# MLP entry of a hybrid encoder layer: the per-row scalars of the norm move off GpSimd, and one form of the residual rows is kept instead of two

## The chip, the core and the metric

One core of a Trainium2 chip runs the whole program. The engines are named as the profile names them: PE (TensorE matmul, with PEld for its weight loads), DVE (VectorE), ACT (ScalarE), POOL (GpSimd), SP (SyncE, which here only issues DMAs). Each engine takes its own instructions strictly in the order in which they stand in the program, and waits where an operand is not ready. The metric is the device time of one execution in microseconds (us); lower is better.

## The reference

One layer on 512 tokens of width 1024, all in float32. The change lies at the joint between its two halves:

```
h = rmsnorm(x, pre_mix_norm)
...                                            # scan branch, window attention, gates
mixed = (g_ssd * y_ssd + g_attn * y_attn) @ w_o
x = x + rmsnorm(mixed, post_mix_norm)          # the residual rows x1
h = rmsnorm(x, pre_mlp_norm)
f = square(relu(h @ w_mlp_in)) @ w_mlp_out
x = x + rmsnorm(f, post_mlp_norm)              # the output
```

with `rmsnorm(x, g) = x * rsqrt(mean(x*x) + 1e-6) * g`, a mean over the 1024 columns of a token. Since the squared ReLU passes a positive factor per token through the MLP (as its square), the kernel need not apply the second rsqrt before the matmuls: any positive scale per token may stand there, if the last norm's epsilon is scaled along. The kernel uses this.

## The kernel before

**Layout.** The 512 tokens are four tiles of 128 rows, t = 0 to 3; a tile of rows of width 1024 is kept as two halves, j = 0, 1, each 128x512. SBUF is handed out in slots of 128x1024 floats, two halves to a slot; names in the profile such as `carved`, `wd`, `h` and `x` are whatever first used a slot.

**Matmuls.** Every float32 operand is split into a high part and a rest (`wh` and `wl` for weights, `b`, `sh` and `sl` for the MLP's activations, `fh` and `fl` for its inner ones), and a product is three matmuls (high with high, rest with high, high with rest), all recorded at line L532; transposes are at L536. ACT makes the high parts (L1811 for MLP weights, L1691 for activations). The rest of an MLP weight is made in one of three ways, chosen per chunk by a string of letters such as `LO_UP`: "v" is one subtraction on DVE (L1820), "p" is four on POOL (also L1820), "d" is a negated copy on ACT (L1815) onto which a DMA issued by POOL adds the weight (L1816).

**The joint.** The output projection `@ w_o` and the MLP's two products are each seven block products of a Strassen-like scheme; its sums and differences of weight blocks are DVE operations (L1772), and one of them is a POOL DMA that adds a weight block from HBM (L1787). As each token tile's rows of `mixed` are complete, `mix_done` runs for it:

- ACT squares and sums the row (L1624); DVE multiplies by the gain (L1625).
- POOL forms `rs`, the factor of the post-mix norm, in three instructions on a 128x1 column (L523, L525, L527), and `rs*rx` in a fourth (L1627), where `rx` (`rst0`) is the token's factor of the very first norm.
- DVE forms `x2 = h2*(rs*rx) + x*rx` (L1629), the residual rows scaled by `rx`, which go through the transposes into the MLP, and `x1 = h2*rs + x` (L1632), the plain residual rows, which SP stores to DRAM (L1637).
- ACT squares and sums x1 (L1636); POOL forms from it, in six instructions on a 128x1 column (L1641 to L1646), `eps2`, the last norm's scaled epsilon.

The x rows are loaded by `load_x` into eight halves, and ACT makes eight scaled copies of them (L1567). The transposed rows are evicted with the gain (L1670 on ACT, L1672 on DVE) and split. Much later `reload_x1` brings x1 back (L1554), and `down_done` forms the last norm from column sums, `eps2`, a Sqrt on ACT (L1999) and a reciprocal on DVE (L2000), and adds x1 (L2013).

**What sets the order.** The program is written in one order, and then a planner (`Planner.plan`) lists the instructions of each engine anew: it plays the program with fixed costs for each kind of instruction, takes for each engine the ready instruction with the earliest due time, and the result is fixed as that engine's order. A few constants steer it: `DUE` is the lead that it gives a POOL DMA, `SPARE_VEC` the margin after an ACT, DVE or POOL result before a matmul that reads it is picked (first number for the part of its played time up to 690 us, second for the rest). Whatever changes costs or dependences can thus move instructions anywhere in the program.

## Time and profile before

| | |
|---|---|
| median of 3 runs | 1050.56 us |
| the runs | 1047.84, 1050.56, 1054.34 us |
| the profiled execution | 1054.07 us, of which 1051.9 us are the span of the profile |
| mean granted PE clock | 0.995 |
| busy in the span | PE 1028.1, DVE 887.2, ACT 687.0, POOL 652.2 us |

The profile's times count from the start of its span; the part outside the span is 2.17 us. Rows of the timeline show start, duration, engine, line, operation, output and inputs, and in brackets how long the engine was idle before and what released it. Rows of waits show who waited for whom: total, number, longest. Rows of windows show for each engine the busy time in a stretch, with the granted PE clock after the counts. Rows of one line show minimum, median and maximum of a duration in ns.

### The profile page before, as it was taken

Reading aid. Unit: us, or ns where it says so; the run is one execution under the profiler, and the core shown is the slowest. Engines: PE = TensorE matmul, PEld = TensorE weight load, DVE = VectorE, ACT = ScalarE, POOL = GpSimd, SP = SyncE. Lnnn points to the kernel's source line nnn. Section 1 sums busy time; section 2 is a strip of 40 time slices with the busy share of each in tenths; the row PEclk is TensorE's granted clock in tenths of the full one; section 3 lists DMA queues with packets and bytes.
Section 4 is the critical chain, followed back from the end, with each engine's and each line's share of the span. In section 5 each row is a group of like instructions: output and inputs, shape, how many; then the busy total and the mean of one; then the engine's idle time right before and its main releaser. Section 6 shows DMA issues by size and latency. Waiting matters only on the chain.

```text
span 1051.9 us, 17148 instructions
## 1 busy us (share of the span) xinstructions
PE 1028.1 (98%) x5812; PEld 886.5 (84%) x5812; DVE 887.2 (84%) x1285; ACT 687.0 (65%) x1277; POOL 652.2 (62%) x733
## 2 busy tenths in 40 slices
PE   9999999999999999999999999998989999999996
PEld 7888888888888888887878888888989999999875
DVE  7688897789995887799989596779978889889998
ACT  5578788768875765656674433778676764846854
POOL 3546657647888998999987487358832244253310
PEclk9999999999999999999999999999989999999999
DMA  7449969979898957749763497776764764864963
GB/s 216 137 139 274 263 151 264 270 178 269 230 248 215 240 166 201 183 140 249 193 148 114 141 352 255 240 239 190 202 148 93 212 152 108 219 144 100 305 154 101
DMA packets 232424, 206.24 MB, mean 196 GB/s; under 512 B 15341, under 2 KB 185557, under 8 KB 232336
## 3 DMA queue, kind: packets, MB, share of 16 engines
q1 hardware_dynamic: 225068, 185.68, 61.8%
q0 software_dynamic: 7120, 19.40, 10.2%
q8 instruction: 46, 0.75, 0.3%
q14 instruction: 42, 0.34, 0.1%
q10 hardware_dynamic: 148, 0.07, 0.0%
HBM read 163.35 MB, written 29.69 MB: 184 GB/s over the span
## 4 chain that ended last, share of the span: by engine, by line
PE 77%; DVE 6%; DMA 6%; POOL 5%; issue 3%; ACT 2%; SPq 2%; DVEq 0%; ACTq 0%; POOLq 0%
PE pp L532 53%; PE ps L532 23%; POOL wl L606 2%; SPq L1032 1%; DVE wl L1820 1%; DMA wd<-in_w_mlp_in 1%; DMA E<-pd 1%; DMA carved<-in_w_mlp_in 1%; POOL eps L1644 1%; DMA pd<-C 1%; DMA post_mlp_norm<-in_post_mlp_norm 1%; DMA bt<-pd 1%; DVE carved L1772 0%; PE ps L536 0%; DMA pd<-t 0%
## 5 line engine op out<-in xcount | busy, mean ns | idle before, releaser
L532 PE MATMUL pp<-b,wh 128*128 128x512 f32 (+1 forms) x1424 | 428.8, 383 | 0.0
L606 POOL TENSOR_TENSOR wl<-wr,wh 128x256 fp32r<-128x256 f32 (+1 forms) x341 | 292.4, 883 | 98.0 <-ACT wh L602 62.1
L532 PEld LDWEIGHTS pp<-b,wh 128*128 128x128 f32 x1424 | 263.4, 189 | 50.8 <-issue 0.9
L532 PE MATMUL pp<-b,wl 128*128 128x512 f32 (+1 forms) x712 | 272.7, 384 | 0.0
L532 PEld LDWEIGHTS pp<-b,wl 128*128 128x128 f32 x712 | 134.8, 190 | 25.7 <-issue 0.2
L602 ACT CAST wh<-wr 128x1024 fp32r<-128x1024 f32 (+1 forms) x99 | 102.7, 1038 | 48.3 <-POOL wl L606 24.8
L532 PE MATMUL ps<-b,wh 128*128 128x256 f32 x400 | 73.2, 285 | 4.0 <-ACT wh L1811 4.0
L532 PE MATMUL pp<-wh,fh 128*128 128x512 f32 x176 | 68.2, 391 | 1.4 <-DVE carved L1975 1.4
L532 PE MATMUL pp<-wl,fh 128*128 128x512 f32 x176 | 68.7, 391 | 0.0
L532 PE MATMUL pp<-wh,fl 128*128 128x512 f32 x176 | 67.9, 389 | 0.0
L532 PEld LDWEIGHTS ps<-b,wh 128*128 128x128 f32 x400 | 62.8, 193 | 5.2 <-ACT wh L1811 4.2
L1820 DVE TENSOR_TENSOR wl<-wd,wh 128x1024 fp32r<-128x1024 f32 x39 | 54.5, 1403 | 13.3 <-ACT wh L1811 10.6
L1811 ACT CAST wh<-carved 128x1024 fp32r<-128x1024 f32 x44 | 46.0, 1048 | 26.3 <-PE ps L532 10.9
L1811 ACT CAST wh<-wd 128x1024 fp32r<-128x1024 f32 x54 | 55.9, 1045 | 10.2 <-POOL rs L1627 2.0
L532 PE MATMUL ps<-b,wl 128*128 128x256 f32 x200 | 55.1, 284 | 0.4 <-DVE wl L1820 0.4
L1816 POOL DMA_DIRECT2D wl<-wd x12 | 10.6, 887 | 68.3 <-ACT wl L1815 34.8
L532 PE MATMUL ps<-sh,wh 128*128 128x256 f32 x160 | 45.0, 283 | 0.0
L532 PE MATMUL ps<-sl,wh 128*128 128x256 f32 x160 | 45.0, 283 | 0.0
L532 PE MATMUL ps<-sh,wl 128*128 128x256 f32 x160 | 44.9, 284 | 0.0
L1820 POOL TENSOR_TENSOR wl<-carved,wh 128x256 fp32r<-128x256 f32 x28 | 32.1, 1206 | 14.4 <-ACT wh L1811 14.4
L532 PE MATMUL pp<-ah,wh 128*128 128x512 f32 x128 | 40.2, 390 | 0.0
L532 PEld LDWEIGHTS pp<-wh,fh 128*128 128x128 f32 x176 | 33.1, 188 | 7.8 <-ACT wh L1811 1.8
(979 smaller groups left out, 2641.9 us busy)
## 6 DMA issues: line engine op xcount, KB each, us to landing
wr<-in_w_in SPq DMA_DIRECT2D x74, 512.0 KB, 5.3
wd<-in_w_mlp_in SPq DMA_DIRECT2D x22, 512.0 KB, 4.3
pd<-t SPq DMA_DIRECT2D x16, 640.0 KB, 6.3
pT<-pd SPq DMA_DIRECT2D x64, 160.0 KB, 5.5
wd<-in_w_mlp_out SPq DMA_DIRECT2D x17, 512.0 KB, 6.6
carved<-in_w_mlp_out SPq DMA_DIRECT2D x17, 512.0 KB, 5.6
wr<-in_w_ssd_out SPq DMA_DIRECT2D x14, 512.0 KB, 5.1
rf<-csT SPq DMA_DIRECT2D x27, 256.0 KB, 6.1
```

The costliest lines, as they stand in the source:

```text
L532: self.nc.tensor.matmul(out, lhsT, rhs, start=start, stop=stop, skip_group_check=more)
L602: self.nc.scalar.copy(hi[:, :m], raw)
L606: engines[e].tensor_tensor(lo[:, c], raw[:, c], hi[:, c].bitcast(F32), op=ALU.subtract)
L1032: nc.sync.dma_start(dst[b * 32:(b + 1) * 32].rearrange("p n a x -> p (n a) x"), d[:, b * 128:(b + 1) * 128].rearrange("(r j) x -> j r x", ...
L1644: tt(e, e, rx, op=ALU.mult)
L1811: nc.scalar.copy(hi, w)
L1816: nc.gpsimd.dma_start(low, w, accum_op=ALU.add)
L1820: (nc.vector if e == "v" else nc.gpsimd).tensor_tensor(low[:, q], w[:, q], hi[:, q].bitcast(F32), op=ALU.subtract)
```

## The change

- `mix_done` has no POOL instruction left. The factor is now formed as `rs*rx` at once: one DVE instruction adds the two column sums and the epsilon, ACT takes a Sqrt with the scale `msd` (the first norm's mean square, over the width), and DVE takes the reciprocal. DVE forms only x2, so one instruction per half instead of two. SP stores x2, ACT squares x2, and the column sums are kept in `sq1`.
- `load_x` scales x in place, so that eight halves of slots are held instead of sixteen.
- `reload_x1` brings x2 back and ACT scales it by `root = 1/rx`, eight new instructions on 128x512.
- `eps2` is formed for all four token tiles at once, in four DVE instructions on 128x4, where the first `down_done` stands. The early `root` Sqrt of the kernel before, which loaded ACT's table for it, is gone; the first Sqrt is now that of `mix_done`.
- `norm_x` keeps the mean square (`ms0`) in a column of its own.
- The constants `DUE`, `SPARE_VEC`, `LO_UP` and `RELU` are set anew: a POOL split of the third up pass becomes a DVE one, and one DVE squared ReLU per pass becomes two ACT instructions. `reload_x1` stands one block product later in the program.

```diff
-DUE = 6000
+DUE = 5000
-LO_UP = "vdvv", "vdvv", "vdvp", "vdvp"
+LO_UP = "vdvv", "vdvv", "vdvv", "vdvp"
-RELU = "vaaaaa"
+RELU = "aaaaaa"
+RELOAD = "D3_1"
-    SPARE_VEC = 500, 800
+    SPARE_VEC = 400, 800
...
     def reload_x1(self):
...
+        nc, root = self.nc, self.const("root", [128, 4])
+        nc.vector.reciprocal(root, self.rst0[:, 0:4])
+        for t in range(NT):
+            for j in range(2):
+                x1 = self.x1[t][j]
+                nc.scalar.activation(x1, x1, AF.Copy, scale=root[:, t:t + 1])
...
     def load_x(self):
...
-            for a, b in zip(self.x2[t], self.x1[t]):
-                self.nc.scalar.activation(a, b, AF.Copy, scale=self.rst0[:, t:t + 1])
+            for a in self.x2[t]:
+                self.nc.scalar.activation(a, a, AF.Copy, scale=self.rst0[:, t:t + 1])
...
     def mix_done(self, t, h2):
...
-        self.rsqrt_mean(rs[:, 0:1], ssq[:, 0:2], D, 4 * EPS)
-        nc.gpsimd.tensor_tensor(rs[:, 1:2], rs[:, 0:1], rx, op=ALU.mult)
+        nc.vector.scalar_tensor_tensor(rs, ssq[:, 0:1], 4 * EPS * D, ssq[:, 1:2], op0=ALU.add, op1=ALU.add)
+        nc.scalar.activation(rs, rs, AF.Sqrt, scale=self.msd[:, t:t + 1])
+        nc.vector.reciprocal(rs, rs)
         for j in range(2):
-            nc.vector.scalar_tensor_tensor(x2[j], h2[j], rs[:, 1:2], x2[j], op0=ALU.mult, op1=ALU.add)
-        for j in range(2):
-            x1 = self.x1[t][j]
-            nc.vector.scalar_tensor_tensor(x1, h2[j], rs[:, 0:1], x1, op0=ALU.mult, op1=ALU.add)
+            nc.vector.scalar_tensor_tensor(x2[j], h2[j], rs, x2[j], op0=ALU.mult, op1=ALU.add)
+            nc.sync.dma_start(self.x1d[t * 128:(t + 1) * 128, j * 512:(j + 1) * 512], x2[j])
...
         for j in range(2):
-            x1 = self.x1[t][j]
-            nc.scalar.activation(junk, x1, AF.Square, accum_out=ssq[:, 2 + j:3 + j])
-            nc.sync.dma_start(self.x1d[t * 128:(t + 1) * 128, j * 512:(j + 1) * 512], x1)
+            nc.scalar.activation(junk, x2[j], AF.Square, scale=D ** -0.5, accum_out=self.sq1[:, j, t:t + 1])
...
-        tt, e = nc.gpsimd.tensor_tensor, self.eps2[:, t:t + 1]
-        tt(e, ssq[:, 2:3], ssq[:, 3:4], op=ALU.add)
-        nc.gpsimd.tensor_scalar(e, e, 1.0 / D, EPS, op0=ALU.mult, op1=ALU.add)
-        tt(e, e, rx, op=ALU.mult)
-        tt(e, e, rx, op=ALU.mult)
-        tt(e, e, e, op=ALU.mult)
-        nc.gpsimd.tensor_scalar(e, e, EPS, None, op0=ALU.mult)
...
     def down_done(self, t, j, col):
...
-            root = self.const("root", [128, 1])
-            nc.scalar.activation(root, self.eps2[:, 0:1], AF.Sqrt)
+            e, rx = self.eps2[:, 0:4], self.rst0[:, 0:4]
+            nc.vector.scalar_tensor_tensor(e, rx, EPS, rx, op0=ALU.mult, op1=ALU.mult)
+            for k in range(2):
+                nc.vector.tensor_tensor(e, e, self.sq1[:, k], op=ALU.add)
+            nc.vector.scalar_tensor_tensor(e, e, EPS, e, op0=ALU.mult, op1=ALU.mult)
```

Since lines are added, the changed kernel's line numbers differ by up to nine from those of the kernel before (L1787 is L1786 there, L1816 is L1815, L1629 is L1639).

First place: POOL's queue in the first and second up pass of the MLP, before. Rows L1816 and L1787 are the two kinds of DMA, `eps` rows the small arithmetic on the token tiles 2 and 3.

```order
L1816 DMA wl_7912<-carved_3731 128x1024
L1645 TENSOR_TENSOR eps_87<-eps_87 128x1
L1646 TENSOR_SCALAR eps_87<-eps_87 128x1
L1816 DMA wl_7786<-carved_3728 128x1024
L1641 TENSOR_TENSOR eps_87<-sq_7570 128x1
L1642 TENSOR_SCALAR eps_87<-eps_87 128x1
L1787 DMA wd_7421<-in_w_mlp_in 128x2x512
L1643 TENSOR_TENSOR eps_87<-eps_87,rst_86 128x1
L1644 TENSOR_TENSOR eps_87<-eps_87,rst_86 128x1
L1645 TENSOR_TENSOR eps_87<-eps_87 128x1
L1646 TENSOR_SCALAR eps_87<-eps_87 128x1
L1787 DMA carved_3728<-in_w_mlp_in 128x2x512
```

The same place on POOL in the changed kernel:

```order
L1815 DMA wl_7565<-wd_7502 128x1024
L1815 DMA wl_7883<-carved_3731 128x1024
L1786 DMA wd_7406<-in_w_mlp_in 128x2x512
L1815 DMA wl_7756<-carved_3732 128x1024
L1786 DMA carved_3732<-in_w_mlp_in 128x2x512
L1815 DMA wl_8004<-carved_3732 128x1024
L1815 DMA wl_8075<-wd_7502 128x1024
```

The DMAs now stand one behind the other; the four `eps` instructions between the two additions of weight blocks are gone, and the addition into `wd` now stands ahead of the last `wl` addition that it followed before.

Second place: DVE's queue where the token tiles 2 and 3 (x_611 and x_612) get their residual rows, before:

```order
L1672 TENSOR_SCALAR carved_3732<-ps_7490,cv 128x256
L1629 SCALAR_TENSOR_TENSOR x_611_7187<-h_650_7531,rs_7534,x_611_7187 128x512
L1629 SCALAR_TENSOR_TENSOR x_611_7187<-h_624_7298,rs_7534,x_611_7187 128x512
L1672 TENSOR_SCALAR carved_3732<-ps_7497,cv 128x256
L1696 TENSOR_TENSOR b_7469<-carved_3732,b_7469 128x512
L1632 SCALAR_TENSOR_TENSOR x_606_7168<-h_650_7531,rs_7534,x_606_7168 128x512
L1696 TENSOR_TENSOR b_7469<-carved_3732,b_7469 128x512
L1629 SCALAR_TENSOR_TENSOR x_612_7190<-carved_3730,rs_7571,x_612_7190 128x512
L1629 SCALAR_TENSOR_TENSOR x_612_7190<-h_624_7298,rs_7571,x_612_7190 128x512
L1632 SCALAR_TENSOR_TENSOR x_606_7168<-h_624_7298,rs_7534,x_606_7168 128x512
```

The same place on DVE in the changed kernel, where the tiles 2 and 3 are x_606 and x_607:

```order
L1635 SCALAR_TENSOR_TENSOR rs_7520<-sq_7519 128x1
L1633 TENSOR_TENSOR h_621_7299<-h_621_7299,post_mix_norm_7181 128x512
L1635 SCALAR_TENSOR_TENSOR rs_7549<-sq_7548 128x1
L1637 RECIPROCAL rs_7520<-rs_7520 128x1
L1633 TENSOR_TENSOR h_621_7299<-h_621_7299,post_mix_norm_7181 128x512
L1637 RECIPROCAL rs_7549<-rs_7549 128x1
L1639 SCALAR_TENSOR_TENSOR x_606_7171<-h_650_7517,rs_7520,x_606_7171 128x512
L1639 SCALAR_TENSOR_TENSOR x_607_7172<-carved_5870,rs_7549,x_607_7172 128x512
L1639 SCALAR_TENSOR_TENSOR x_606_7171<-h_621_7299,rs_7520,x_606_7171 128x512
L1639 SCALAR_TENSOR_TENSOR x_607_7172<-h_621_7299,rs_7549,x_607_7172 128x512
L1695 TENSOR_TENSOR b_7454<-carved_3734,b_7454 128x512
```

The second form of the rows (L1632) is gone, two short DVE instructions per token tile have come in ahead of the rows, and both tiles' rows now stand in front of the split of `b`.

Third place: ACT's queue in the last down pass of the changed kernel, where rows L1563 are the new rescaling of reloaded rows, L1810, L1814 and L1726 the casts for the matmuls:

```order
L1726 CAST fh_10561<-s_976_10401 128x1024
L1563 ACTIVATE ag_10452<-ag_10452,root 128x512
L1814 ACTIVATE wl_10396<-carved_3732 128x1024
L1810 CAST wh_10395<-carved_3732 128x1024
L1563 ACTIVATE x_989_10469<-x_989_10469,root 128x512
L1814 ACTIVATE wl_10462<-wt_10459 128x1024
L1810 CAST wh_10461<-wt_10459 128x1024
```

In the kernel before the same casts stand there with nothing between them; the rescaling now shares the queue with them.

More of the change, by code (lines that the diff above doesn't have):

```diff
@@ L700, in start @@
         self.rst0 = self.const("rst0", [128, 4])
-        self.eps2 = self.const("eps2", [128, 4])
+        self.sq1 = self.const("sq1", [128, 2, 4])
+        self.eps2, self.ms0, self.msd = (self.const(n, [128, 4]) for n in ("eps2", "ms0", "msd"))
         nc.vector.memset(one, 0.0)
@@ L756, in norm_x @@
         nc.vector.tensor_tensor_reduce(junk[1], x[1], x[1], 1.0 / D, EPS, ALU.mult, ALU.add, ssq[:, 1:2])
-        nc.gpsimd.tensor_tensor(r, ssq[:, 0:1], ssq[:, 1:2], op=ALU.add)
-        nc.gpsimd.tensor_tensor(r, r, self.mhalf, op=ALU.pow)
+        m = self.ms0[:, t:t + 1]
+        nc.gpsimd.tensor_tensor(m, ssq[:, 0:1], ssq[:, 1:2], op=ALU.add)
+        nc.gpsimd.tensor_tensor(r, m, self.mhalf, op=ALU.pow)
         tok = slice(t * 128, (t + 1) * 128)
@@ L1554, in reload_x1 @@
                 self.nc.sync.dma_start(x1, self.x1d[t * 128:(t + 1) * 128, j * 512:(j + 1) * 512])
+        nc, root = self.nc, self.const("root", [128, 4])
[4 more added lines that the diff above has]
+                nc.scalar.activation(x1, x1, AF.Copy, scale=root[:, t:t + 1])
     def load_x(self):
         self.x1d = self.dp.tile([512, 1024], F32, name="x1d")
-        self.x1 = [[self.slots.get("x1") for _ in range(2)] for _ in range(NT)]
+        self.x1 = [[None] * 2 for _ in range(NT)]
+        self.x2 = {t: [self.slots.get("x2") for _ in range(2)] for t in range(NT)}
         for t in range(NT):
             for j in range(2):
-                self.nc.sync.dma_start(self.x1[t][j], self.d_x[0, t * 128:(t + 1) * 128, j * 512:(j + 1) * 512])
+                self.nc.sync.dma_start(self.x2[t][j], self.d_x[0, t * 128:(t + 1) * 128, j * 512:(j + 1) * 512])
         self.g2 = self.norm_rows("post_mix_norm")
-        self.x2 = {}
+        self.nc.vector.tensor_scalar(self.msd, self.ms0, 1.0 / D, None, op0=ALU.mult)
         for t in range(NT):
-            self.x2[t] = [self.slots.get("x2") for _ in range(2)]
-            for a, b in zip(self.x2[t], self.x1[t]):
-                self.nc.scalar.activation(a, b, AF.Copy, scale=self.rst0[:, t:t + 1])
+            for a in self.x2[t]:
+                self.nc.scalar.activation(a, a, AF.Copy, scale=self.rst0[:, t:t + 1])
     def held_back(self, fn):
@@ L1618, in mix_done @@
         nc = self.nc
-        ssq, rs = self.tmp("sq", [128, 4], 4), self.tmp("rs", [128, 2], 4)
-        rx = self.rst0[:, t:t + 1]
+        ssq, rs = self.tmp("sq", [128, 2], 4), self.tmp("rs", [128, 1], 4)
         self.h2t[t] = x2 = self.x2.pop(t)
@@ L1625, in mix_done @@
             nc.vector.tensor_tensor(h2[j], h2[j], self.g2[j], op=ALU.mult)
[L1626 to L1627 removed]
+        self.slots.put(junk)
+        nc.vector.scalar_tensor_tensor(rs, ssq[:, 0:1], 4 * EPS * D, ssq[:, 1:2], op0=ALU.add, op1=ALU.add)
+        nc.scalar.activation(rs, rs, AF.Sqrt, scale=self.msd[:, t:t + 1])
+        nc.vector.reciprocal(rs, rs)
         for j in range(2):
[L1629 removed]
+            nc.vector.scalar_tensor_tensor(x2[j], h2[j], rs, x2[j], op0=ALU.mult, op1=ALU.add)
+            nc.sync.dma_start(self.x1d[t * 128:(t + 1) * 128, j * 512:(j + 1) * 512], x2[j])
+        self.slots.put(*h2)
+        junk = self.slots.get("junk")
         for j in range(2):
[L1631 to L1646 removed]
+            nc.scalar.activation(junk, x2[j], AF.Square, scale=D ** -0.5, accum_out=self.sq1[:, j, t:t + 1])
+        self.slots.put(junk)
         if t == 3:
@@ L2069, in build @@
             p, i = int(name[1]), int(name[3])
-            if name == "D3_0":
+            if name == RELOAD:
                 self.at(n() + 1, self.reload_x1)
```

2 lines of the change are left out of this document (removed).

## The prediction

> **What bounds the kernel now.** I read the page's busy line and slices first.
>
> ```profile
> PE 1028.1 (98%) x5812; PEld 886.5 (84%) x5812; DVE 887.2 (84%) x1285; ACT 687.0 (65%) x1277; POOL 652.2 (62%) x733
> PE   9999999999999999999999999998989999999996
> PEclk9999999999999999999999999999989999999999
> ```
>
> PE is busy for 98% of the span, so no engine's total work matters, only the places where PE stands still or runs slowly: two weak slices before three quarters of the span, the second with a lower granted clock, and the end. The windows around the first two:
>
> ```profile
> 720.00:740.00 20.00, 17.42 (x142) 16.90 (x143) 19.92 (x26) 17.20 (x29) 16.45 (x18) 1.00 0.65 178
> 740.00:760.00 20.00, 20.00 (x169) 20.00 (x168) 19.59 (x21) 14.45 (x19) 19.26 (x8) 1.00 0.73 193
> 772.80:778.33 5.53, 5.49 (x25) 5.49 (x26) 3.97 (x3) 2.87 (x4) 5.07 (x4) 0.50 0.26 48
> 780.00:1000.00 220.00, 220.00 (x1390) 199.97 (x1389) 196.25 (x177) 148.33 (x179) 83.09 (x80) 1.00 0.65 169
> ```
>
> (Busy columns: PE, PEld, DVE, ACT, POOL; then the clock.) From 780 to 1000 us PE never stops. In the entry, DVE is full for 40 us (39.51 of 40), and after the last stall PE runs 5.5 us at half clock. The waits from 700 to 790 us name the stalls:
>
> ```profile
> PE ps L532 <- ACT wh L1811: 4.0, 1, 4.0
> DVE x L1629 <- POOL rs L1627: 1.8, 1, 1.8
> PE pp L536 <- DVE hr L1672: 1.5, 1, 1.5
> PE pp L536 <- ACT wh L1811: 1.3, 1, 1.3
> PE ps L532 <- DVE wl L1820: 0.4, 1, 0.4
> ```
>
> PE loses 4.0 us once and 1.3 + 1.5 + 0.4 = 3.2 us before. The timeline, taken engine by engine, gives the reason for the large one:
>
> ```profile
> 742.78 1.26 POOL L1787 DMA_DIRECT2D wd<-in_w_mlp_in  x1 [0.36 <-DVE fr L1756]
> 745.64 13.16 POOL L1646 TENSOR_SCALAR eps<-eps 128x1 f32<-128x1 f32 x1
> 758.85 1.25 POOL L1787 DMA_DIRECT2D carved<-in_w_mlp_in  x1
> 764.92 1.06 ACT L1815 ACTIVATE wl<-carved 128x1024 fp32r<-128x1024 f32 x1 [6.26 <-DMA carved<-in_w_mlp_in]
> 772.84 0.58 PE L532 MATMUL ps<-b,wh 128*128 128x256 f32 x1 [4.04 <-ACT wh L1811]
> ```
>
> One POOL instruction on 128 numbers lasts 13.16 us. Behind it stands the DMA that adds a weight block; ACT waits 6.26 us for its landing, with nine casts and activations queued behind up to the one that PE needs, and PE waits for the last of the casts. Why 13 us:
>
> ```profile
> 744.88 0.68 DVE L1756 TENSOR_TENSOR fr<-fr,ps 128x512 f32<-128x512 f32 x1
> 745.64:758.80 13.16, 13.16 (x112) 13.16 (x111) 13.16 (x14) 10.45 (x14) 13.16 (x1) 1.00 0.81 230
> 758.64 0.68 DVE L1756 TENSOR_TENSOR carved<-carved,pp 128x512 f32<-128x512 f32 x1
> ```
>
> DVE runs 14 instructions without a gap, and none between 745.48 and 758.64 reads PSUM (`pp` or `ps`). POOL ends when one does. The smaller stalls have the same source:
>
> ```profile
> 711.69 5.92 POOL L1644 TENSOR_TENSOR eps<-eps,rst 128x1 f32<-128x1 f32 x1
> 714.23 0.19 ACT L1624 ACTIVATION_READ_ACCUMULATOR h<-h 128x1 f32 x1
> 718.29 0.19 POOL L523 TENSOR_TENSOR rs<-sq 128x1 f32<-128x1 f32 x1
> 719.75 1.42 DVE L1629 SCALAR_TENSOR_TENSOR x<-h,rs,x 128x512 f32<-128x512 f32 x2 [1.79 <-POOL rs L1627]
> ```
>
> Tile 2's sums are done at 714.4, but tile 1's `eps2` holds POOL until `rs` can begin at 718.29; DVE waits for it, and PE's 1.3 us end with the rows that DVE then writes.
>
> The Trainium skill (SBUF — State Buffer, Who interferes with whom) says that a DVE instruction with two SBUF inputs and a GpSimd one that reads SBUF exclude each other, the second blocked until the first finishes. By that a POOL row would pay about one DVE instruction, 1.2 us, not the 13.16 us measured over 14 of them; with 1.2 us there would be no stall here to win. The trace decides.
>
> **The change part by part.** Durations from these rows:
>
> ```profile
> L1632 DVE SCALAR_TENSOR_TENSOR x<-h,rs,x x3: 741/744/745, 722.1 to 736.8; 128x512 f32<-128x512 f32 x3
> L2002 DVE SCALAR_TENSOR_TENSOR frs<-fsq,eps x4: 151/152/154, 1033.6 to 1037.9; 128x1 f32<-128x1 f32 x4
> L1999 ACT ACTIVATE frs<-fsq,frs x4: 278/294/295, 1037.9 to 1043.9; 128x1 f32<-128x1 f32 x4
> 704.31 0.75 DVE L1629 SCALAR_TENSOR_TENSOR x<-carved,rs,x 128x512 f32<-128x512 f32 x1
> 705.82 0.38 PE L536 MATMUL ps<-ident,x 128*128 128x128 f32 x2
> 732.78 1.28 ACT L1988 ACT_TABLE_LOAD   x1
> 734.08 0.20 ACT L1988 ACTIVATE root<-eps 128x1 f32<-128x1 f32 x1
> L1567 ACT ACTIVATE x<-x,rst x4: 707/708/710, 673.5 to 686.4; 128x512 f32<-128x512 f32 x4
> L1787 POOL DMA_DIRECT2D wd<-in_w_mlp_in x6: 1208/1225/1258, 742.8 to 933.7; - x6
> ```
>
> *The large stall.* Without the eps rows, carved's DMA no longer waits 13 us behind them: it issues once DVE's difference (T1) and the `wl` addition ahead of it in the new order are done. I expect it about 10 us earlier (estimate: 13.16 less the addition's own transfer), and ACT's 6.26 us wait goes whole. The cast that ended at about 772.8 would then end at 766.5, before PE needed it at 768.8. Gain 4.04 us, and with it the half clock: 5.49 us of matmuls at 0.50 would take 2.75 us, gain 2.75. Bounds: 0 and 6.8; I take all, since what is late next on ACT has 2.3 us (768.8 - 766.5) in hand.
>
> *The small stalls.* POOL's chain for `rs` becomes DVE, ACT, DVE. At the median durations that is 0.15 + 0.29 + 0.15 = 0.6 us and three hand-overs, against the 5.3 us that pass from 714.4 to 719.75. The rows also come in another queue order: both instructions of a tile now hold what stands behind them on DVE, ACT's Sqrt holds the casts behind it. DVE's load in the entry falls by 8 x 0.74 = 5.9 us (L1632) and rises by 8 + 3 short instructions x 0.15 = 1.7 us, net 4.2 us less on the engine that was full. I take 2.8 of the 3.2 us; bounds 0 and 3.2, and below nothing in the first rival.
>
> *The Sqrt table.* One load before (at 732.78), one now, in front of tile 0's factor. It starts while DVE forms the sum. Tile 0's rows came only at 704.3 before, behind another split, and PE's first transposes at 705.8; with the rows' durations laid along the new queue I have the rows of tiles 0 and 1 ready at about 705.0. Cost nothing, cover 0.8 us. The Trainium skill (ScalarE: Activation LUTs, What ACT_TABLE_LOAD costs) counts 2.66 us for a switch, a 1.38 us drain behind the 1.28 us load; here the next instruction starts 0.02 us after the load's end. By the page the cover would be overrun by 0.6 us.
>
> *Slots, loads, stores.* Four whole slots come free before the entry. Eight loads of x, eight stores and eight reloads remain, 256 KB each. SP's stores now carry x2, ready no later than x1 was. Nothing on PE's path: cost 0; a gain by earlier weight loads is bounded by the same 3.2 us.
>
> *Letters.* Three of 14 rests of the third up pass move from POOL to DVE (3 x 1.2 us), four squared ReLUs (0.7 us) from DVE to two ACT instructions each. In 780 to 1000 PE is at 220.00 of 220 us with DVE at 196 and ACT at 148: hidden. Were that cover gone, it is 3.6 us on DVE.
>
> *The end.* Eight rescalings of 0.71 us, 5.7 us, enter ACT's queue among the casts of the last down pass.
>
> ```profile
> 1013.00:1036.00 23.00, 21.64 (x96) 17.64 (x95) 22.30 (x28) 14.90 (x22) 2.57 (x3) 1.00 0.36 68
> DMA to landing us min/median/max: 5.9/7.9/9.2
> PE pp L532 <- DVE carved L1975: 1.4, 1, 1.4
> ```
>
> (The second row is that of the reloads, L1554.) ACT has 23.00 - 14.90 = 8.1 us free there, more than 5.7, and the reloads' place in SP's queue, behind the last weight load, is what it was. PE's one wait there, 1.4 us, is for DVE. Cost 0.6 us, an estimate of one cast pushed by one rescaling; bounds 0 and 5.7.
>
> *The first 700 us.* `SPARE_VEC` and the changed dependences reorder PE there too: the same matmuls in other places. PE's waits between 16 and 700 us are few:
>
> ```profile
> PE ps L532 <- ACT bth L549: 2.1, 3, 1.5
> PE ps L532 <- DVE xh L550: 0.8, 1, 0.8
> PE ps L532 <- ACT x L1275: 0.5, 1, 0.5
> PE ps L532 <- ACT xh L549: 0.4, 1, 0.4
> ```
>
> Sum 3.8 us: at best that is won, and as much may be lost. I take 0.
>
> **Sum.** -4.04 - 2.75 - 2.8 + 0.6 = -9.0 us. Against the profiled execution: 1054.07 - 9.0 = 1045.1 us. That execution was 3.5 us above the median of the runs (1050.56). If the runs differ by this stall's length, they all fall to 1045; if by something else, the median falls to 1041.6. I take the first as likelier, since a POOL instruction that waits for a hole in DVE's work is a thing of chance, and say **1044.5 us**.
>
> **The rivals.**
>
> *DVE becomes the bound.* It was full from 720 to 760, and the new chain makes DVE wait for ACT twice per tile. The small stalls then stay, and only the large one goes: 1054.07 - 6.8 + 0.6 = 1047.9 us. Against it: net 4.2 us less DVE work. Chance 0.15.
>
> *The reload blocks ACT (slower).* ACT's first L1563 stands ahead of four casts of the last pass. If its row lands later than ACT gets there (about 1013), ACT stands with the casts behind it. At the median landing of 7.9 us, with the 8.1 - 5.7 = 2.4 us that ACT has left, PE waits 5.5 us, and after that runs as long at half clock as here, 2.75 us: 1054.07 - 9.6 + 8.3 = 1052.8 us, above the median before. For it: the reload stands one block product later in the program. Against it: SP's queue order, and the last reload before issued at 1003. Chance 0.12.
>
> *POOL's DMAs stay late.* If DVE holds up the issue of a POOL DMA as it held its arithmetic, the change removes the arithmetic and not the wait: about 1051 us, the small stalls alone won (1054.07 - 2.8). Against it: L1787 took 1208 to 1258 ns six times, the one at 742.78 beside a full DVE. The Trainium skill (SBUF — State Buffer, SBUF: two separate sides) warns of just this, for DVE instructions in a two-port mode; by it the sum would be this rival's 1051 us, and the six durations speak against it. Chance 0.05.
>
> *The reordered first part costs or wins.* 4 to 15 us lost, around 1052 us and up to 1060: chance 0.08. Its 3.8 us won besides, 1040 to 1041 us: chance 0.1.
>
> **How the numbers follow.** The forecast itself, 1041 to 1047, has 0.5. The range that holds 8 in 10 reaches from 1039 (all waits gone, the sum taken from the median) to 1054 (the slower rival with its bound). About 1% is what a measurement of this kernel can tell from no change: faster than 1040.05 needs the whole gain below the median and some of the first part, 0.17; slower than 1061.07 needs a long loss by reordering, 0.06; the rest, 0.77, is within 1%.
>
> **What would show it.** In the profile of the changed kernel: no POOL row on a 128x1 column between 700 and 760 us; the addition into the second weight block (L1786 there) issued before about 752; ACT's 6.3 us wait and PE's 4.0 us wait gone, and no stretch at half clock before the end; PE's waits between 715 and 730 below 0.5 us; DVE below 19.9 of 20 us after 720. The forecast is wrong if a new PE wait of over 2 us stands anywhere, first of all behind L1563 after 1010 us or in the first 700 us.

## The result, and the profile after

The changed kernel takes 1042.94 us (median of 6 runs, 1042.19 to 1044.93) against 1051.57 us for the kernel before (6 runs, 1047.84 to 1054.34): a ratio of 0.9925, 95% interval 0.9902 to 0.9948. Its profiled execution took 1044.93 us, with a span of 1043.1 us; profile against profile that is 9.1 us less, median against median 8.6 us. In the later sets of runs, one of the kernel before (1463.36 us) and one of `small_gone` (2082.66 us) were far slower than all others of their kernel and are left out of medians and ratios.

The page of the changed kernel, busy line and slices:

```profile
PE 1024.5 (98%) x5812; PEld 883.1 (85%) x5812; DVE 877.9 (84%) x1290; ACT 695.4 (67%) x1296; POOL 597.5 (57%) x681
PE   8999999999999999998999999999999999999996
PEclk9999999999999999999999999999999999999999
```

The two weak slices before three quarters of the span and the lower clock are gone. The windows of the entry and of the long middle (busy PE, PEld, DVE, ACT, POOL, then the clock):

```profile
720.00:740.00 20.00, 20.00 (x171) 20.00 (x170) 19.55 (x23) 18.68 (x31) 3.54 (x4) 1.00 0.65 154
740.00:760.00 20.00, 20.00 (x169) 20.00 (x168) 18.89 (x23) 17.36 (x25) 2.11 (x2) 1.00 0.90 246
760.00:780.00 20.00, 20.00 (x148) 19.03 (x147) 16.54 (x16) 16.35 (x22) 8.36 (x7) 1.00 0.81 176
780.00:1000.00 220.00, 218.83 (x1368) 198.10 (x1367) 188.64 (x177) 144.74 (x173) 67.66 (x68) 1.00 0.65 164
```

PE is full through the entry, DVE no longer is, and POOL has next to nothing to do. What does stand out is the last row: the middle, where PE never stopped before, now has 1.2 us of idle PE. PE's longest waits behind the first 10 us:

```profile
PE ps L533 <- ACT bth L550: 1.8, 2, 1.5
PE ps L533 <- DVE acc L1974: 1.5, 2, 0.9
PE ps L533 <- ACT x L1278: 1.4, 1, 1.4
PE pp L533 <- DVE wl L1819: 1.2, 1, 1.2
```

None is in the entry. The first and the third lie in the first 700 us, the second at the end, and the last is the new one in the middle, which ends at 946.71 us. The chain that was late before, in the timeline of POOL, DVE and ACT:

```profile
735.30 1.23 POOL L1786 DMA_DIRECT2D wd<-in_w_mlp_in  x1 [7.70 <-ACT fr L1753]
748.41 1.21 POOL L1786 DMA_DIRECT2D carved<-in_w_mlp_in  x1 [9.68 <-ACT carved L1753]
717.23 0.15 DVE L1635 SCALAR_TENSOR_TENSOR rs<-sq 128x1 f32<-128x1 f32 x1
717.42 0.30 ACT L1636 ACTIVATE rs<-rs,msd 128x1 f32<-128x1 f32 x1 [0.15 <-DVE rs L1635]
717.97 0.15 DVE L1637 RECIPROCAL rs<-rs 128x1 f32<-128x1 f32 x1
718.71 0.73 DVE L1639 SCALAR_TENSOR_TENSOR x<-h,rs,x 128x512 f32<-128x512 f32 x1
```

The addition into `carved` is issued at 748.41 instead of 758.85, and POOL, which held it up before, now stands idle for 9.68 us until ACT lets it go on. ACT still waits for its landing, 1.13 us instead of 6.26, because the landing took 8.4 us instead of 6.0. In a second profile of the changed kernel it took 10.2 us, and the chain from the addition over ACT to PE shows again, without any small POOL row (POOL, then ACT's and PE's waits):

```profile
749.03 1.21 POOL L1786 DMA_DIRECT2D carved<-in_w_mlp_in  x1 [10.21 <-DMA wl<-carved]
ACT wl L1814 <- DMA carved<-in_w_mlp_in: 3.4, 1, 3.4
PE ps L533 <- ACT wh L1810: 1.2, 1, 1.2
```

The factor of tile 2 is ready 0.9 us after DVE starts on it (717.23 to 718.12).

**A ledger.** To compare whole kernels I add up, for every matmul in a trace, the time to the next matmul's start less the median of that time for its width. The sum is what PE lost in a stretch, slow clock included; the last column is the time from the last matmul to the end of the span. All in us, one profiled execution each; the kernels of the lower rows are the experiments below. A single profile is a rough sample: `before`, `eps_late`, `small_gone` and `eps_twice` have nearly the same order of instructions up to 690 us and yet lose 18.8 to 21.4 us in the first 700. The profile of `code_alone` is its slowest run of twelve (1049.04 us, median 1044.65), with two stretches of 3.4 us at half clock, at 12 and 541 us; that of `consts_alone` (1049.93 us, median 1046.95) has one, at 186 us.

| kernel | 0-700 | 700-740 | 740-780 | 780-1000 | 1000 on | after PE | span |
|---|---|---|---|---|---|---|---|
| before | 21.4 | 4.5 | 6.7 | 0.4 | 2.3 | 9.5 | 1051.9 |
| before, second profile | 20.6 | 3.7 | 6.3 | 0.2 | 2.5 | 9.5 | 1050.0 |
| after | 22.9 | 0.0 | 0.0 | 1.9 | 2.4 | 8.8 | 1043.1 |
| after, second profile | 22.9 | 0.0 | 1.6 | 0.4 | 2.4 | 8.9 | 1043.3 |
| `eps_late` | 20.4 | 1.5 | 0.3 | 0.3 | 2.1 | 9.4 | 1041.2 |
| `eps_back` | 23.1 | 0.0 | 0.0 | 0.4 | 2.4 | 9.3 | 1042.3 |
| `code_alone` | 26.5 | 1.5 | 0.0 | 1.1 | 3.2 | 7.9 | 1047.2 |
| `consts_alone` | 25.2 | 3.2 | 0.2 | 0.3 | 2.1 | 9.7 | 1047.8 |
| `rows_gone` | 22.9 | 1.3 | 1.1 | 1.0 | 3.3 | 8.1 | 1044.8 |
| `small_gone` | 18.8 | 2.2 | 0.2 | 0.3 | 2.1 | 9.6 | 1040.4 |
| `eps_twice` | 19.6 | 7.9 | 0.1 | 0.4 | 2.4 | 9.6 | 1047.1 |

So the entry (700 to 780) gave 11.2 us, and 2.4 us went back elsewhere: 1.5 in the first 700 us, 1.5 in the middle, 0.1 at the end, less 0.7 behind the last matmul. Together that is the 8.8 us between the spans.

### The profile page after: what moved, and what is told of

Read it like the earlier page. It is cut to its first block, busy times and chain, and to the rows that moved or that the text cites. A ratio compares the mean times of both kernels' runs of the same rounds, so it can differ in the third digit from the quotient of the medians.

```text
span 1043.1 us, 17101 instructions
## 1 busy us (share of the span) xinstructions
PE 1024.5 (98%) x5812; PEld 883.1 (85%) x5812; DVE 877.9 (84%) x1290; ACT 695.4 (67%) x1296; POOL 597.5 (57%) x681
## 4 chain that ended last, share of the span: by engine, by line
PE 90%; DMA 4%; POOL 2%; DVE 2%; ACT 1%; issue 1%; SPq 0%; DVEq 0%; ACTq 0%; POOLq 0%
PE pp L533 62%; PE ps L533 26%; POOL wl L607 1%; DMA wr<-in_w_in 1%; DMA wd<-in_w_mlp_out 1%; PE ps L537 1%; DMA rstd<-rrow 1%; DMA E<-pd 1%; DMA carved<-pd 0%; DMA x<-in_x 0%; DVE ag L2010 0%; DMA rrow<-rcol 0%; SPq L1035 0%; DVE carved L2015 0%; DVE x L2015 0%
## 5 line engine op out<-in xcount | busy, mean ns | idle before, releaser
L1819 DVE TENSOR_TENSOR wl<-wd,wh 128x1024 fp32r<-128x1024 f32 x40 | 52.8, 1326 | 13.9 <-ACT wh L1810 10.9
L1810 ACT CAST wh<-carved 128x1024 fp32r<-128x1024 f32 x47 | 49.0, 1047 | 20.8 <-PE ps L533 7.9
L1810 ACT CAST wh<-wd 128x1024 fp32r<-128x1024 f32 x51 | 52.7, 1044 | 5.4 <-DMA wd<-in_w_mlp_out 2.8
L1815 POOL DMA_DIRECT2D wl<-carved x13 | 11.6, 895 | 70.9 <-ACT wl L1814 52.6
L1815 POOL DMA_DIRECT2D wl<-wd x9 | 8.5, 942 | 62.4 <-ACT wl L1814 36.1
L533 PE MATMUL pp<-yh,wh 128*128 128x512 f32 x128 | 39.7, 391 | 0.0
```

The costliest lines, as they stand in the source:

```text
L533: self.nc.tensor.matmul(out, lhsT, rhs, start=start, stop=stop, skip_group_check=more)
L1810: nc.scalar.copy(hi, w)
L1815: nc.gpsimd.dma_start(low, w, accum_op=ALU.add)
L1819: (nc.vector if e == "v" else nc.gpsimd).tensor_tensor(low[:, q], w[:, q], hi[:, q].bitcast(F32), op=ALU.subtract)
```

## The experiments

Theory: small POOL arithmetic is locked out beside DVE and holds up POOL's own DMAs. Rivals: DVE's load in the entry was the limit; the constants and the order bring the gain. The first four kernels ran on one chip beside 35 runs of the kernel before (median 1049.22 us), the next four on another beside 31 (1050.24 us). After every edit the planner lists the instructions anew, so no run keeps the order of the entry fixed; that the order itself moves the entry is a rival that stays.

### The eps rows alone taken out: `eps_late`

```diff
 mix_done, before:
-        tt, e = nc.gpsimd.tensor_tensor, self.eps2[:, t:t + 1]
-        ...                                  # the six rows
 down_done, first call:
+            nc.vector.tensor_tensor(e, self.sq1[:, 0], self.sq1[:, 1], op=ALU.add)
+            nc.vector.tensor_scalar(e, e, 1.0 / D, EPS, op0=ALU.mult, op1=ALU.add)
+            ...                              # twice times rx, then EPS * e * e
```

> The kernel before with one part of the change: the six GpSimd rows per tile that form eps2 are gone, the two sums go to a constant, and five VectorE rows of 128x4 form eps2 where it is used. Both row sets x1 and x2, the GpSimd chain for the factor, the slots, the reload and all constants stay as before. Theory (GpSimd's small arithmetic is starved beside VectorE and delays its own DMA): the 13.16 us row is gone, carved's addition is issued about 10 us earlier, ACT's 6.3 us wait, PE's 4.0 us and the half clock go, and part of the small stalls; five rows of 0.15 us come at the end: 1043 to 1045.5 us, 6 to 8 us faster. Rival (VectorE's load in the entry was the limit, and its eight rows of 0.74 us stay here): no more than 2 us faster, 1048.5 or above. Rival (order and constants): no change, 1050 to 1052.

Measured: 1044.55 us, ratio 0.9947 (0.9921 to 0.9973). From its timeline on POOL:

```profile
712.13 3.12 POOL L523 TENSOR_TENSOR rs<-sq 128x1 f32<-128x1 f32 x1 [8.09 <-ACT h L1625]
741.22 1.19 POOL L1781 DMA_DIRECT2D carved<-in_w_mlp_in  x1 [0.51 <-DVE wt L1766]
```

The addition into `carved` is issued 17.6 us earlier, and the ledger's entry falls from 11.2 to 1.8 us, with all of DVE's rows still there. That is the theory's result, and the load of DVE cannot be what held the entry. But 17.6 us is more than the 13.16 us of the row that is gone: the entry's new order has a share in it that was not separated. One row of the factor's chain still waits 3.12 us.

### The eps rows put back into the changed kernel: `eps_back`

```diff
 mix_done, after:
+        tt(e, rx, rx, op=ALU.mult)
+        ts(e, e, EPS, None, op0=ALU.mult)
+        tt(e, e, q[:, 0:1], op=ALU.add)
+        tt(e, e, q[:, 1:2], op=ALU.add)
+        tt(e, e, e, op=ALU.mult)
+        ts(e, e, EPS, None, op0=ALU.mult)
```

> The changed kernel with the small GpSimd arithmetic put back: eps2 is formed again tile by tile by six GpSimd rows of 128x1 in the entry (from the same two sums), and not at the end. Everything else as changed. Theory: each chain waits for a hole in VectorE's work, so single rows of 3 to 13 us stand on GpSimd between 705 and 760, the DMAs queued behind them issue late, and ACT and PE wait again: 1047 to 1053 us. Rival (less VectorE work, one row set): 1043 to 1044.5, with the rows short or long but nothing waiting for them. Rival (order and constants): 1043 to 1044.5.

Measured: 1044.38 us, ratio 0.9942 (0.9918 to 0.9966). My theory, as I had put it, missed: 24 small POOL rows stand in the entry again and cost nothing that can be measured. Its longest row, and the addition:

```profile
727.59 1.30 POOL L1650 TENSOR_TENSOR eps<-eps,sq 128x1 f32<-128x1 f32 x1
748.15 1.20 POOL L1794 DMA_DIRECT2D carved<-in_w_mlp_in  x1 [9.45 <-ACT sh L1698]
```

The last eps row ends at 730.05, not at 758.8, since in the new order and without the x1 rows the squares come earlier, and no eps row lasts over 1.3 us. A small POOL row is not dear in itself; it is dear where it falls.

### The code without the constants, and the constants without the code

```diff
 code_alone (after):                      consts_alone (before):
-DUE = 5000                              -DUE = 6000
+DUE = 6000                              +DUE = 5000
 ...  LO_UP, RELU, SPARE_VEC and RELOAD as before   ...  LO_UP, RELU, SPARE_VEC as after
```

> The changed kernel with the constants of before: DUE 6000, LO_UP with two p rests, RELU with its v, RELOAD D3_0, SPARE_VEC 500. Theory: the gain is the code's, so 1042 to 1046 us; the first 700 us may come out up to 3 us better, since SPARE_VEC orders them as before. Rival (the replanned constants bring the gain): 1048 to 1052.

> The kernel before with the changed constants alone: DUE 5000, LO_UP, RELU, SPARE_VEC 400 (RELOAD has nothing to act on). Theory: the GpSimd rows stay and starve, so 1049 to 1054 us as before, with single 128x1 rows of 5 us and more in the entry. Rival (the constants bring the gain): 1042 to 1046.

Measured: `code_alone` 1044.65 us, 0.9947 (0.9922 to 0.9972); `consts_alone` 1046.95 us, 0.9970 (0.9945 to 0.9995). The code brings the gain by itself. The side guess did not come true: with `SPARE_VEC` 500 the first 700 us lost 26.5 us, and less the two stretches at half clock (some 3.4 us, an estimate: half of twice 3.4) still 23.1, no better than the 22.9 of the changed kernel. The constants alone fall between both expectations: somewhat faster, by another road than either theory said. On POOL and in PE's waits:

```profile
714.08 5.91 POOL L1643 TENSOR_TENSOR eps<-eps,rst 128x1 f32<-128x1 f32 x1
751.08 1.17 POOL L1646 TENSOR_SCALAR eps<-eps 128x1 f32<-128x1 f32 x1
752.29 1.25 POOL L1787 DMA_DIRECT2D carved<-in_w_mlp_in  x1
PE ps L532 <- ACT x L1275: 2.9, 1, 2.9
```

One row is still locked out, but tile 3's last ones meet another order on DVE, last at most 1.17 us each, and the addition goes out in time; against that, a wait of 2.9 us at 183 us that was 0.5 before, with 3.4 us at half clock behind it. So an order alone can clear the late addition, with all small rows still on POOL.

### The two halves of the change, one at a time

`small_gone` is `eps_late` with the factor's chain also off POOL; `rows_gone` is the code of the changed kernel with both chains left on POOL, the constants of before, and one Sqrt on a scratch column where the first `down_done` stands.

```diff
 small_gone, in mix_done before:
-        self.rsqrt_mean(rs[:, 0:1], ssq[:, 0:2], D, 4 * EPS)
-        nc.gpsimd.tensor_tensor(rs[:, 1:2], rs[:, 0:1], rx, op=ALU.mult)
+        nc.vector.scalar_tensor_tensor(rs[:, 0:1], ssq[:, 0:1], 4 * EPS * D, ssq[:, 1:2], op0=ALU.add, op1=ALU.add)
+        nc.scalar.activation(rs[:, 0:1], rs[:, 0:1], AF.Sqrt, scale=1.0 / D)
+        nc.vector.reciprocal(rs[:, 0:1], rs[:, 0:1])
+        nc.vector.tensor_tensor(rs[:, 1:2], rs[:, 0:1], rx, op=ALU.mult)
 rows_gone, in mix_done after (and the six eps rows of eps_back):
-        nc.vector.scalar_tensor_tensor(rs, ssq[:, 0:1], 4 * EPS * D, ssq[:, 1:2], op0=ALU.add, op1=ALU.add)
-        nc.scalar.activation(rs, rs, AF.Sqrt, scale=self.msd[:, t:t + 1])
-        nc.vector.reciprocal(rs, rs)
+        self.rsqrt_mean(rs, ssq, D, 4 * EPS)
+        nc.gpsimd.tensor_tensor(rs, rs, self.rst0[:, t:t + 1], op=ALU.mult)
```

> The changed kernel once more, unchanged, so that it stands beside the next three on one chip. Low VectorE load in the entry, no small GpSimd arithmetic there. All theories: 1042 to 1045 us, 6 to 9 us under the kernel before.

> The first half of the change alone: both row sets stay (VectorE's eight rows more), but no small GpSimd arithmetic is left in the entry: the factor goes over VectorE and ACT, eps2 is formed at the end. Constants of before. Theory 1: 1042 to 1046 us, as fast as the changed kernel within 2 us, since nothing can starve. Theory 2: the same, the GpSimd rows being gone; it differs only in rows_gone. Theory 3 (VectorE's load sets the entry): 1047 to 1050, with PE waiting for VectorE at 715 to 760.

> The other half of the change alone: only the rows x2 are kept and stored (eight VectorE rows of 0.74 us less, fewer slots), but all small arithmetic stays on GpSimd: four rows per tile for the factor, six for eps2. Constants of before. Theory 1 (the small GpSimd rows starve by chance, wherever they stand): 1046 to 1052 us, with single rows of 3 us and more and a late addition into carved. Theory 2 (a row starves for long only where VectorE runs two-input work without a hole, and the eight rows that are gone leave holes and bring the last squares, so the last eps rows, some 12 us earlier, in front of the DMAs that matter): 1042 to 1046.5 us, GpSimd rows of 1 us at most after 725, no wait of ACT above 2 us. Theory 3 (the factor's chain is what holds VectorE): the waits of the small stalls at 715 to 730 stay, 1045 to 1048.

Measured, beside each other: `small_gone` 1042.75 us, 0.9937 (0.9913 to 0.9960); the changed kernel again 1043.79 us, 0.9943 (0.9921 to 0.9965); `rows_gone` 1047.19 us, 0.9967 (0.9945 to 0.9989). The window 700 to 780 of the kernel before, of `small_gone` and of `rows_gone`, in this order (busy PE, PEld, DVE, ACT, POOL):

```profile
700.00:780.00 80.00, 72.69 (x534) 69.26 (x533) 69.51 (x83) 57.36 (x92) 55.87 (x52) 0.96 0.68 181
700.00:780.00 80.00, 78.71 (x595) 75.16 (x595) 78.79 (x106) 65.30 (x106) 15.10 (x14) 1.00 0.74 199
700.00:780.00 80.00, 78.45 (x596) 75.29 (x596) 71.53 (x83) 64.73 (x105) 35.72 (x45) 1.00 0.74 209
```

With only the small arithmetic gone, DVE is fuller than ever (78.79 of 80 us) and PE has its matmuls on time: 595 in the window against 534. So the whole gain of the change is in this half. The other half alone also clears most of the entry (no small POOL row over 1.47 us), but is 3.1 us faster than before where `small_gone` is 7.5. Theory 1's long rows did not come; theory 2 had the short rows nearly right (1 us at most) but missed an ACT wait of 2.4 us for the addition into `wd`, and the time is 0.7 us above its range; theory 3's range holds the time, but of its stalls on PE only one of 0.7 us is left.

By the ledger the difference between the two halves is not lost in the entry (2.4 us in both) but before it, 22.9 against 18.8. All kernels that keep one set of rows lose 22.9 to 23.1 us in the first 700 (`code_alone` without its half clock), those with both sets and the constants of before 18.8 to 21.4. The changed constants put into the kernel before cost there too (25.2, some 1.7 of it half clock). PE's waits there are not the same in all of them: one of 1.2 to 1.5 us before 184.7 us and one of about 1.4 at 485 stand in the changed kernel and in `eps_back`, and of 2.9 and 1.3 in `consts_alone`, all with `SPARE_VEC` 400; with 500 they are at most 0.7. `rows_gone` and `code_alone` have one of 2.1 and 2.4 us at 538 to 540 instead. Both the constant and the single set seem to have a price there; the single profiles do not settle how much is whose.

### More of the same: `eps_twice`

```diff
 mix_done, before:
+        for e in (self.twice[:, t:t + 1], self.eps2[:, t:t + 1]):
             ...                              # the six rows, once into a scratch column
```

> The kernel before with its six eps rows per tile done twice (the second set into a scratch column), 24 GpSimd rows more beside a full VectorE. Theories 1 and 2: each of them can lose its stretch of VectorE's work, so the addition into carved comes later still: 3 to 10 us slower than before, 1052 to 1060, with several rows of 3 us and more. Rival (the rows are not what delays GpSimd's DMAs): within 1.5 us of before; at 0.2 us a row they add only 5 us to an engine that is 62% busy.

Measured: 1050.85 us, ratio 1.0011 (0.9989 to 1.0034): no change, as the rival had it. Its long rows on POOL, the addition, and PE's largest wait:

```profile
708.37 7.18 POOL L1644 TENSOR_SCALAR eps<-eps 128x1 f32<-128x1 f32 x1
724.45 4.61 POOL L1646 TENSOR_TENSOR eps<-eps,rst 128x1 f32<-128x1 f32 x1
755.10 1.25 POOL L1789 DMA_DIRECT2D carved<-in_w_mlp_in  x1 [0.56 <-DMA wl<-carved]
PE pp L536 <- ACT fr L1756: 4.1, 1, 4.1
```

Twice as many rows, but two over 4 us instead of three; the others last up to about 1.3 us. The 4.1 us stall has moved to 717 us, to the rows of tiles 2 and 3; the later one is absent, although the addition is only 3.8 us earlier, since PE and ACT come to that place later as well. The number of rows does not set the loss.

### A second profile of the kernel before

> The kernel before, unchanged, for a second profile. Its 67 times fall into two groups, about 1045 to 1048 and 1050 to 1056 us, some 5 to 6 us apart, about as much as the large stall with its half clock (6.8 us). Theory: the groups are the runs without and with a long lock-out of tile 3's last eps rows. If this run comes out under 1048.5, no eps row lasts over 8 us, the addition into carved is issued before about 754, and PE's 4 us wait and the half clock are absent; if it comes out above 1050, all of them are there as in the first profile. Rival (the groups come from the first 700 us, from memory, or from the clock): the entry looks alike in both, with its 4 us wait, whichever the time.

Measured: 1052.15 us. In the timeline of POOL and PE's waits:

```profile
710.16 5.92 POOL L1644 TENSOR_TENSOR eps<-eps,rst 128x1 f32<-128x1 f32 x1
729.14 5.62 POOL L1645 TENSOR_TENSOR eps<-eps 128x1 f32<-128x1 f32 x1
744.13 13.16 POOL L1646 TENSOR_SCALAR eps<-eps 128x1 f32<-128x1 f32 x1
PE ps L532 <- ACT wh L1811: 4.0, 1, 4.0
```

The same rows last as long as in the first profile to 0.01 us, and the time lies above 1050, as the theory had it; the rival allows that too. Of 31 times on one chip, 12 lie from 1044.8 to 1048.1 and 19 from 1050.1 to 1054.6. Both profiles are of the upper group, so the long row is no accident there; no run of the lower group was profiled, and whether it has the long row is not shown. Each run's mean granted clock is on record: it is 0.995 in the two profiled executions, in which the stretch at half clock follows the stall, 0.997 or more in 6 of the 12 and in 2 of the 19. So a part of the lower group seems to run without that stretch, which speaks for the theory and does not prove it.

### The lock-out by itself: three small programs

```python
def two(o):  nc.vector.tensor_tensor(o, a, b, op=ALU.mult)                 # two inputs in SBUF
def rows(o): nc.vector.scalar_tensor_tensor(o, a, g, b, ...)               # with a column g as scalar
def psum(o): nc.vector.tensor_tensor(o, a, bank, op=ALU.mult)              # one input in PSUM
def one(o):  nc.vector.tensor_scalar(o, a, 0.5, None, op0=ALU.mult)        # one input
# beside them, once in a stage:
nc.gpsimd.tensor_tensor(e[:, 0:1], f[:, 0:1], f[:, 1:2], op=ALU.add)
```

> A program of its own that computes none of the layer (it writes zeros): one short GpSimd addition of 128x1 is issued while VectorE or ScalarE runs ten or more instructions of 128x512 without a gap, in a stage for each kind, and what the GpSimd row lasts is read. Theory (GpSimd reads SBUF only in a hole of VectorE's two-input work): beside ten products of two SBUF tiles (0.68 us each) the row lasts about 6 us, beside twenty about 13 us, beside ten scaled additions (0.74 us) about 7 us; with one VectorE instruction that reads PSUM as the fifth it ends there, after about 3 us; beside ten with PSUM input, beside ten ScalarE copies and on its own 0.1 to 0.3 us; six chained rows beside twenty products all end only after the last, and beside a mix of three products and one PSUM read they need several of the holes; a 128x512 addition of GpSimd is pushed out as well. Rival (blocked only until the instruction that holds the port ends): 0.3 to 1.0 us in every stage, however many VectorE instructions follow. Rival (the long rows come of a semaphore or of queueing, not of memory): about the same in all stages. A GpSimd DMA beside twenty products issues in 1.2 us by both.

> A program of its own again (none of the layer, it writes zeros), to see whether the short GpSimd row's wait is a draw. 16 stages for each kind of VectorE work: one GpSimd addition of 128x1 is issued beside 14 VectorE instructions without a gap, the first of them 96, 122, ... 486 columns wide, the other 13 with 512, so that GpSimd's request meets the next boundary between two VectorE instructions 26 columns later each time. If it is a draw on the moment of the request: some of the 16 rows beside products of two SBUF tiles last under 0.7 us, some the whole stretch, about 8 us, and nearly nothing between; beside scaled additions the same with 9 us; beside products with PSUM all 0.2 to 0.3 us; beside one-input instructions, which took 0.33 us each, some to the stretch's end, 4 us. If the row merely waits for the instruction in hand: all under 0.8 us. If it is always starved: all 8 to 9 us.

> A third program of its own (none of the layer, zeros written). The two before it left a question: beside the same products a short GpSimd addition lasted 0.2 to 0.6 us in stages that VectorE began after a pause, and to the end of the stretch (8 us) in stages that it ran into from the stage before. Here every stage begins after a pause of VectorE of about 2 us; it then runs k + 12 products of two SBUF tiles (0.60 us apart) without a break, and the GpSimd addition asks when product k is done, k = 0, 1, 2, 4, 6, 8, 10, 12, 16, 20, 24, 28. If a pause lets GpSimd in and a long unbroken stretch locks it out: up to some k the row lasts under 0.7 us, from there it lasts the remaining 11 products, about 6.5 us; where the change comes is what is measured. If the moment of the request decides and not the pause: all rows alike, all short or all long. Then, for k = 4, 12 and 20: a product with a PSUM operand two instructions ahead of the request (if a hole resets the lock, these are short at every k; if not, as the first set); a scaled addition with a column as scalar four instructions behind the request (if it lets GpSimd in, the long rows end there, after about 2.5 us; if not, 8 us); a PSUM operand four behind it (ends there, about 2.3 us, by every theory).

From the first program, POOL beside ten and beside twenty products, beside ten with PSUM, ten with one input, and the first and the next five of a chain beside twenty products:

```profile
6.41 0.58 POOL L56 TENSOR_TENSOR two_eps<-two_first 128x1 f32<-128x1 f32 x1 [1.10 <-DVE two_first L49]
13.10 12.01 POOL L56 TENSOR_TENSOR two_eps<-two_first 128x1 f32<-128x1 f32 x1 [6.11 <-DVE two_first L49]
43.63 0.19 POOL L56 TENSOR_TENSOR psum_eps<-psum_first 128x1 f32<-128x1 f32 x1 [9.12 <-DVE psum_first L49]
50.27 3.33 POOL L56 TENSOR_TENSOR one_eps<-one_first 128x1 f32<-128x1 f32 x1 [6.45 <-DVE one_first L49]
60.74 0.57 POOL L56 TENSOR_TENSOR six_eps<-six_first 128x1 f32<-128x1 f32 x1 [5.88 <-DVE six_first L49]
61.39 2.93 POOL L58 TENSOR_TENSOR six_eps<-six_eps,six_first 128x1 f32<-128x1 f32 x5
```

Both answers occur beside the same products: one instruction's time (0.58 us), or the whole stretch (12.01 us of 20 products). That refutes both the theory as a rule (10 products, 6 us) and the rival. The second program tried 16 moments of the request: beside products the rows lasted 0.19 to 0.74 us and about 8 us strictly in turn, whatever the moment, so it is no draw either. (Its 16 stages of scaled additions all began after a pause of VectorE and their rows lasted 0.20 to 0.61 us, not 9; they tell nothing of a long stretch.) What went in turn was how VectorE came into the stage (DVE, POOL, DVE, POOL):

```profile
12.83 0.75 DVE L43 SCALAR_TENSOR_TENSOR two_first<-a,g,b 128x512 f32<-128x512 f32 x1
13.66 7.99 POOL L50 TENSOR_TENSOR two_eps<-two_first 128x1 f32<-128x1 f32 x1 [7.92 <-DVE two_first L43]
21.92 0.75 DVE L43 SCALAR_TENSOR_TENSOR two_first<-a,g,b 128x512 f32<-128x512 f32 x1 [0.32 <-ACT g L47]
22.75 0.19 POOL L50 TENSOR_TENSOR two_eps<-two_first 128x1 f32<-128x1 f32 x1 [1.10 <-DVE two_first L43]
```

After a pause (0.32 us idle) the row gets in; in a stretch that runs on from the stage before it does not. The third program sets the time since the pause: first the last short and the first long row of the plain stages, then a PSUM product two instructions ahead of the request, a scaled addition four behind it, and a PSUM product four behind it:

```profile
30.39 0.58 POOL L51 TENSOR_TENSOR p__eps<-p__key 128x1 f32<-128x1 f32 x1 [10.13 <-DVE p__key L30]
42.30 6.60 POOL L51 TENSOR_TENSOR p__eps<-p__key 128x1 f32<-128x1 f32 x1 [11.34 <-DVE p__key L30]
204.90 7.20 POOL L51 TENSOR_TENSOR h__eps<-h__key 128x1 f32<-128x1 f32 x1 [5.31 <-DVE h__key L30]
256.88 1.78 POOL L51 TENSOR_TENSOR r__eps<-r__key 128x1 f32<-128x1 f32 x1 [5.31 <-DVE r__key L30]
312.67 1.78 POOL L51 TENSOR_TENSOR f__eps<-f__key 128x1 f32<-128x1 f32 x1 [12.00 <-DVE f__key L30]
```

A request 2.0 us after the pause still gets in at the next boundary; one 3.2 us after it, and all eight later ones (to 17.7 us), wait to the end of the stretch, 6.60 us. A PSUM read that lies behind the request does not help (7.20 us); one that comes, or a scaled addition that comes, lets the row in as it starts (1.78 us, three products after the request). All three lines are the same at k = 4, 12 and 20.

## Why the prediction was right, and where it was not

- **Large stall and half clock (4.04 + 2.75 us).** The addition went out 10.4 us earlier (said: about 10), no slow clock, and the ledger's 740 to 780 goes from 6.7 to 0.0. One step was too good: ACT's wait was to go whole, but the landing took 8.4 and 10.2 us in the two profiles instead of 6.0, and ACT still waited 1.1 and 3.4 us. In the first the cover on ACT was enough; in the second PE waited 1.2 us and lost 1.6 in all. The DMA engines were busier meanwhile (0.94 and 0.78 of the time from issue to landing, against 0.67 before); whether that is the reason is not shown.
- **Small stalls (2.8 of 3.2 us).** Right in kind, too small: 700 to 740 goes from 4.5 to 0.0. I had counted PE's waits, 3.2 us; by the ledger 1.2 to 1.3 us more were lost between matmuls around them. My count of new short DVE instructions, 8 + 3, was off (`mix_done` has 8, the other six stand outside the entry), by 0.5 us of load and without effect on the sum.
- **The Sqrt table (0).** Right. Its cover, by my reckoning, was thin; the rows of tiles 0 and 1 came at 706.5 instead of 705.0, in a profile that by the ledger is 1.5 us later at 700, and PE lost nothing between 700 and 712.

```profile
700.76 1.28 ACT L1636 ACT_TABLE_LOAD   x1
702.06 0.29 ACT L1636 ACTIVATE rs<-rs,msd 128x1 f32<-128x1 f32 x1
```

- **The letters (0).** Too small: I called 780 to 1000 covered because PE was at 220.00 of 220. It lost 1.5 us there, most of it in the 1.2 us wait for a weight rest on DVE (L1819) that ends at 946.71; in the second profile that wait is absent (0.4 us in all), so its cover is thin rather than gone. That the letters are the reason is not shown: `code_alone` and `rows_gone`, with the letters of before, lose 1.1 and 1.0 us there, `eps_back`, with the new ones, 0.4.
- **The end (0.6 us).** 0.1 us more lost on PE and 0.7 us less behind its last matmul: the rescalings lie wholly beside other work.
- **The first 700 us (0).** 1.5 us worse, within the bounds given. The two halves put it down to the single set of rows or, by the waits at 184 and 485 us, to `SPARE_VEC`, not to the small arithmetic; it is no more than profiles of one order differ by.
- **The sum.** Predicted -9.0; measured -8.8 between the spans and -9.1 between the profiled executions. It came as -11.2 in the entry and +2.4 elsewhere, against my -9.6 and +0.6: two errors that cancelled, so that it fits to 0.2 us is luck.
- **The median.** I said 1044.5, on the ground that the long row is "a thing of chance", that the runs before differ by it and that all would fall to 1045. The row repeats to 0.01 us in the two profiles before; since both are of the upper group, the ground is neither shown nor refuted. The median came out at 1042.9, between 1045 and the 1041.6 that I had worked out for the other case. The account above is that of the upper group: on the chip of those 31 times the changed kernel (1043.79) is 8.5 us faster than the upper group's median (1052.3) and 3.3 us faster than the lower group's (1047.1), and where the lower group saves the difference is open.
- **The rivals.** DVE as the bound is refuted by `small_gone`. No wait of ACT or PE stands behind L1563. POOL's DMAs went out on time. The reordered first part cost 1.5 us, not 4 or more. Of the signs that I had named, all came but the end of ACT's wait, of which 1.1 us are left: no 128x1 row on POOL, the addition before 752, no wait of PE from 715 to 730, DVE at 19.55 of 20 after 720; the new wait stayed under 2 us.

The mechanism held in its core and needed two corrections. That DVE's two-input work locks POOL out until a PSUM read comes is shown by the third program. A scaled addition with a column as its scalar frees it as well, which the first profile of the kernel before could have told me (POOL, then DVE):

```profile
730.66 5.62 POOL L1645 TENSOR_TENSOR eps<-eps 128x1 f32<-128x1 f32 x1
736.14 0.74 DVE L1632 SCALAR_TENSOR_TENSOR x<-carved,rs,x 128x512 f32<-128x512 f32 x1
```

The row ends at 736.28, as the scaled addition starts. (A `scalar_tensor_tensor` without a column, the squared ReLU at 756.90 us, did not end the 13.16 us row.) And nothing of it happens within about 2 us of a pause of DVE. The Trainium skill (SBUF — State Buffer, Who interferes with whom) has the second engine wait until the first instruction finishes; the runs agree after a pause (0.57 us) and differ by the length of the stretch otherwise (12.01 us).

So the cause is narrower than the change: taking the small arithmetic off POOL is enough, and the reduction to one set of rows, rescaled on reload, adds nothing that could be measured on top (0.9943 with it, 0.9937 without). It is not the only way: `eps_back`, `rows_gone` and `consts_alone` clear most of the entry with small rows on POOL, in another order. What the traces show is the lock-out and the addition behind it; how much of each gain is the missing rows and how much the new order was not separated.

## What to carry to other kernels

In these traces a POOL instruction on 128 numbers cost 0.2 us, the time of one DVE instruction, or as much as DVE's unbroken stretch lasted, so look in the timeline for POOL rows far longer than their size, see what is queued behind them, and move the arithmetic or its place rather than count the rows. When a change has two halves, run each by itself: here one alone gave all of the gain. And check a term set to zero "because the engine is full" by what that fullness hides, since two small errors can cancel in a sum that comes out right.
